# One address phase for all weights, and 256-column products in the gate and the second output half

## The chip, the core and the metric

The kernel runs on one core of a Trainium2 chip. The metric is the device time of one execution, in microseconds (us). TensorE (PE in the profile) multiplies: each product is a weight load (PEld) of a 128 x 128 block and a MATMUL that streams an operand of up to 512 columns past it into PSUM. VectorE is DVE, ScalarE is ACT, GpSimd is POOL, SyncE is SP. SBUF is the on-chip memory of 128 partitions; addresses here are bytes within a partition.

## What is computed

Two layers of an encoder on 256 positions of width 2048, in float32. Cut to what matters:

```python
for i in range(DEPTH):                       # 2
    u = _rmsnorm(h, norm_g[i]) @ w_in[i]     # 2048 -> 5632
    a_val, a_glu, a_z, q, k, v, b_z = jnp.split(u, offs, axis=-1)
    ya = _conformer_conv(a_val, a_glu, ...) * jax.nn.silu(a_z)
    yb = _window_attention(q, k, v, bias_band, sink[i]) * jax.nn.silu(b_z)
    h = h + jnp.concatenate([ya, yb], axis=-1) @ w_out[i]
    e = _rmsnorm(p[i] @ w_pe[i], pe_g[i])
    h = h + e * jax.nn.sigmoid(h @ w_pg[i])
return _rmsnorm(h, final_g)
```

## The kernel before

Activations are kept transposed: features on the partitions in 16 tiles of 128, the 256 positions along the free dimension. To keep float32 accuracy with the fast float32r products, every operand is held as two parts, `hi` (the value cast to float32r) and `lo` (what the cast left over), and a product is the sum of three: w_hi x_hi, w_hi x_lo and w_lo x_hi. The operand tiles (`hg` for the normed input, `ya` and `yb` for the two head groups, `h1` for the residual) have the shape [128, 2, 8, 256]: hi and lo, eight feature tiles, 256 positions.

The weights stream from HBM in halves of [128, 1024] float32, 156 a layer. Two halves come with one DMA (`load`, on SP). `split` (lines 163 to 172) turns one half into a `w` tile that holds hi (ACT, line 169) and then lo (DVE, line 172), up to `LS` = 4 halves ahead of their use. There are five such buffers, one for each tag `w0` to `w4`, used in turn; each is 2 x 1024 + 16 elements long, 8256 bytes, and the data begin `SHIFT[i]` elements after its start, with `SHIFT = (0, 2, 4, 8, 16)` (line 52). Half h uses the tag h modulo 5. The allocator puts the five buffers one after another, `w4` first, at a multiple of 64 bytes; the operand tiles are 16384 bytes each.

`step` (line 420) takes the next half, runs its eight slices of 128 x 128 through `mm3`, and then calls `pump`, which issues what is due of the side work: convolution taps on DVE, one stage of an attention head, and so on. Side work therefore stands between the steps on every engine, in an order that is fixed by the program for DVE, PE and ACT.

`mm3` (line 398) has two forms. With a two-dimensional output it makes three products of 256 columns (lines 405 to 407). With a three-dimensional output it makes two (lines 402 and 403): w_hi against hi and lo side by side, 512 columns into a whole PSUM bank, and w_lo against hi, 256 columns, into the bank's second half. In this wide form the two halves of the bank must be added afterwards.

A layer runs: `e` (the embedding, `w_pe`), `ag` (value and gate of the convolution), `k`, `v`, then for each pair of head tiles `zb` and `q`, with attention as side work, then `za`, the output projection and the gate. Attention's own products are the scores (line 648), the transposes (line 675) and probabilities times values (line 685). The layernorm of the convolution group adds products at lines 724, 355 and 369 while the first half of the output projection runs.

The output projection is done in two passes. The first takes the attention half of the weights (`yb`) in the narrow form, two output tiles to a bank, and adds the bank into `az` (line 772). The second takes the convolution half (`ya`) in the wide form, a bank for each output tile, with two adds each (line 784), and splits the result into `h1` (lines 785 and 786).

The gate (`w_pg`) uses the wide form through `wide` (line 445); `merge` (line 409) adds the halves of a bank, an ACT copy (line 413) and a DVE add (line 414), and `gate` (line 800) applies the sigmoid, multiplies, adds and squares. Only the last tile of the last layer was already in the narrow form. `pair` (line 438), the narrow form for two tiles in one bank, serves the input projection.

Of the kernel before, what the change touches and what calls it, by code (L numbers as in the profile page):

```python
# [10 lines left out]
F32 = mybir.dt.float32  # L11
F32R = mybir.dt.float32r
# [5 lines left out]
P = 128  # L18
D = 2048
S = 256  # L20
DEPTH = 2
KT = D // P
# [16 lines left out]
HALF = 1024  # L39
# [9 lines left out]

NB_FIRST = KT  # L50
NSPL = 5
SHIFT = (0, 2, 4, 8, 16)
MAN = 'DVE,PE,Activation'
LY = (2, 1)
ORD = 1
# [74 lines left out]
def trunk_kernel(ctx: ExitStack, tc: tile.TileContext, xT, pT, wst, par, gain, relb, sinkp, onehot, out):  # L130
    nc = tc.nc
# [2 lines left out]
        ctx.enter_context(tc.manual_schedule(engines={getattr(ET, x) for x in MAN.split(",")}))  # L134
    big = ctx.enter_context(tc.tile_pool(name="big", bufs=5))
    wraw = ctx.enter_context(tc.tile_pool(name="wraw", bufs=3))
    wspl = ctx.enter_context(tc.tile_pool(name="wspl", bufs=1))
    cst = ctx.enter_context(tc.tile_pool(name="cst", bufs=1))
    wk = ctx.enter_context(tc.tile_pool(name="wk", bufs=2))
    ps = ctx.enter_context(tc.tile_pool(name="ps", bufs=8, space=PSUM))  # L140
# [2 lines left out]
    def bigt(name, dt=F32):  # L143

        return big.tile([P, 2, 8, S], dt, tag="big", name=name)

    def halves(t):
        return [t[:, 0], t[:, 1]]

    def bank(name):  # L150
        return ps.tile([P, 2, S], F32, tag="ps", name=name)
# [10 lines left out]

    def split(h):
        raw = raws[h // 2][:, h % 2, :]
        i = h % NSPL
        w = wspl.tile([P, 2 * HALF + 16], F32R, tag=f"w{i}", name=f"w{h}")
        w = w[:, SHIFT[i]:SHIFT[i] + 2 * HALF].rearrange("p (t n) -> p t n", t=2)
        hi, lo = w[:, 0], w[:, 1]
        nc.scalar.copy(hi, raw)  # L169
        spl[h] = w  # L170
        if h not in (4, 5):
            nc.vector.tensor_sub(lo, raw, hi.bitcast(F32))  # L172
# [17 lines left out]
    def get(h):  # L190

        r = h % NHALF
        if r < 12:
            ahead(h + (r | 1) + 2 - r)
        else:
            ahead(h + LS)
        return spl.pop(h)
# [31 lines left out]
    def later(f, *args):  # L229

        def g():
            f(*args)
            return
            yield

        side.append(g())
# [43 lines left out]
    h = halves(bigt("x"))  # L280
# [104 lines left out]
    def square_acc(acc, src, first, eng=None):  # L385

        if first:
            nc.scalar.activation(acc, src, AF.Square)
            return
        sq = wk.tile([P, 2, S], F32, name="sq", tag="sq", bufs=3)  # L390
        nc.scalar.activation(sq, src, AF.Square)
        (eng or nc.gpsimd).tensor_add(acc, acc, sq)
# [5 lines left out]
    def mm3(o, w, x, start, stop):  # L398


        if len(o.shape) == 3:
            nc.tensor.matmul(o, w[:, 0], x, start=start, stop=False, skip_group_check=True)  # L402
            nc.tensor.matmul(o[:, 1], w[:, 1], x[:, 0], start=False, stop=stop, skip_group_check=True)  # L403
            return
        nc.tensor.matmul(o, w[:, 0], x[:, 0], start=start, stop=False, skip_group_check=True)  # L405
        nc.tensor.matmul(o, w[:, 0], x[:, 1], start=False, stop=False, skip_group_check=True)  # L406
        nc.tensor.matmul(o, w[:, 1], x[:, 0], start=False, stop=stop, skip_group_check=True)  # L407

    def merge(bs):

        t = wk.tile([P, 2, S], F32, name="hl", tag="ptt")[:, 0:len(bs), :]
        for x, b in enumerate(bs):
            nc.scalar.copy(t[:, x, :], b[:, 1, :])
            nc.vector.tensor_add(t[:, x, :], b[:, 0, :], t[:, x, :])
        return t

    class Cursor:
        h = 0

    def step(o, X, start, stop):  # L420

        steps([o], X, [start], stop)

    def steps(os, X, starts, stop):

        parts = []
        for _ in os:
            name, _, k0, nk = HALVES[Cursor.h % NHALF]
            parts.append(get(Cursor.h).rearrange("p t (k c) -> p t k c", k=nk))
            Cursor.h += 1  # L430
        for kk in range(nk):
            k = k0 + kk
            for o, w, start in zip(os, parts, starts):
                mm3(o, w[:, :, kk, :], X[k // 8][:, :, k % 8, :], start and kk == 0, stop and kk == nk - 1)
        for _ in os:
            pump()

    def pair(X, name):
        b = bank(name)
        for x in range(2):  # L440
            step(b[:, x, :], X, x == 0, False)
            step(b[:, x, :], X, False, True)
        return b

    def wide(X, name):

        b = bank(name)
        step(b, X, True, False)
        step(b, X, False, True)
        return b  # L450

    def hilo(hi, lo, src):
# [5 lines left out]
    for l in range(DEPTH):  # L458
# [28 lines left out]
        for q in range(4):  # L487
            n = Cursor.h
            Cursor.h += 1
            if l:  # L490
                w = get(n).rearrange("p t (j k c) -> p t j k c", j=4, k=2)
            else:
                raw = raws[n // 2][:, n % 2, :].rearrange("p (j k c) -> p j k c", j=4, k=2)
            for jj in range(0, 4, 2):
                j = 4 * q + jj
                b = bank("e")
                for x in range(2):
                    for k in range(2):
                        if l:
                            mm3(b[:, x, :], w[:, :, jj + x, k, :], pp[:, :, k, :], x == 0 and k == 0, k == 1)  # L500
                        else:
                            nc.tensor.matmul(b[:, x, :], raw[:, jj + x, k, :], pf[:, k, :], start=x == 0 and k == 0,
                                             stop=k == 1, skip_group_check=True)
# [89 lines left out]
        for ts in FIRST_TILES:  # L593
            bs = [bank(f"ag{l}_{t}") for t in ts]
# [14 lines left out]
        b = pair(hg, f"k{l}")  # L609
# [9 lines left out]
        for q in range(4):  # L619
            n = Cursor.h  # L620
            Cursor.h += 1
            w = get(n).rearrange("p t (k c) -> p t k c", k=4)
# [67 lines left out]
        for i in range(0, 8, 2):  # L690

            b = pair(hg, f"zb{l}_{i}")
            nc.scalar.activation(zb[:, i:i + 2, :], b, AF.Silu)
            b = pair(hg, f"q{l}_{i}")

            qq = wk.tile([P, 2, 2, S], F32R, name="qq", tag="qq")
            for hh in range(2):
                r, o = rows_of[hh], rows_of[1 - hh]
# [7 lines left out]
        for t in range(0, NCT, 2):  # L706
            b = pair(hg, f"za{l}_{t}")
# [55 lines left out]
        Y = [ya, yb]  # L763
        for k in (0, 4):
            nc.gpsimd.dma_start(zb[:, k:k + 4, :], hsrc[:, 8 + k:12 + k, :])
        h1 = []
        for j in range(0, KT, 2):
            b = bank(f"o{l}_{j}")
            for x in range(2):
                step(b[:, x, :], Y, x == 0, True)  # L770
            d = az[:, j // 8, j % 8:j % 8 + 2, :]
# [3 lines left out]
        for j in range(0, KT, 2):  # L775
            d = az[:, j // 8, j % 8:j % 8 + 2, :]
            if j % 8 == 0:
                h1.append(bigt(f"h1{l}_{j // 8}", F32R))
            hi, lo = (x[:, j % 8:j % 8 + 2, :] for x in halves(h1[-1]))
            for x in range(2):  # L780
                b = bank(f"o{l}_{j + x}")
                step(b, Y, True, True)
                for y in range(2):
                    nc.vector.tensor_add(d[:, x, :], b[:, y, :], d[:, x, :])
            nc.scalar.copy(hi, d)
            sub = lambda d=d, hi=hi, lo=lo: nc.vector.tensor_sub(lo, d, hi.bitcast(F32))
            if j < KT - 2:
                later(sub)
            else:
                sub()  # L790
# [3 lines left out]
        last = l == DEPTH - 1  # L794
# [5 lines left out]
        def gate(j, b):  # L800

            i, jj, n = j // 8, j % 8, b.shape[1]
            hh, hl = (x[:, jj:jj + n, :].bitcast(F32) for x in halves(h1[i]))
            hs = wk.tile([P, 2, S], F32, name="hs", tag="u", bufs=3)[:, 0:n, :]
            nc.vector.tensor_add(hs, hh, hl)
            sg = wk.tile([P, 2, S], F32, name="sg", tag="sq", bufs=3)[:, 0:n, :]
            nc.scalar.activation(sg, b, AF.Sigmoid)
            d = e[i][:, jj:jj + n, :]
            nc.vector.tensor_mul(d, d, sg)
            nc.vector.tensor_add(d, d, hs)  # L810
            if n == 2:
                square_acc(hacc, d, j == 0)
            else:
                sq = wk.tile([P, 2, S], F32, name="sq", tag="sq", bufs=3)[:, 0, :]
                nc.scalar.activation(sq, d[:, 0, :], AF.Square)
                if j == KT - 1:
                    hparts.append(sq)
                else:
                    hparts.append(fold(hacc))
                    nc.vector.tensor_add(hparts[0], hparts[0], sq)  # L820
            if last:
                for x in range(n):
                    nc.scalar.activation(og[i][:, jj + x, :], e[i][:, jj + x, :], AF.Copy,
                                         scale=gcol(DEPTH, j + x))
            elif jj + n == 8:
                nc.gpsimd.dma_start(hscr[:, 8 * i:8 * i + 8, :], e[i])
# [4 lines left out]
        hparts = []  # L831
        for j in range(0, KT - 2, 2):
            if j:
                bs = [wide(h1, f"g{l}_{j + x}") for x in range(2)]
            else:
                bs = [bank(f"g{l}_{x}") for x in range(2)]
                for n in range(2):
                    for b in bs:
                        step(b, h1, n == 0, n == 1)
            gate(j, merge(bs))  # L840
            if j == 4 and not last:
                pp = wk.tile([P, 2, 2, S], F32R, name="pp", tag="qq")
                hilo(pp[:, 0], pp[:, 1], pf)
        for j in range(KT - 2, KT):
            if last and j == KT - 1:
                b = bank(f"g{l}_{j}")[:, 0:1, :]
                step(b[:, 0, :], h1, True, False)
                step(b[:, 0, :], h1, False, True)
                gate(j, b)
            else:  # L850
                gate(j, merge([wide(h1, f"g{l}_{j}")]))
        drain()
        h = e

# [7 lines left out]
    for j in (0, 2, 12, 4, 6, 14, 8, 10):  # L862
        for x in [slice(0, 1), slice(1, 2)] if j == 0 else [slice(0, 2)]:
            d = og[j // 8][:, j % 8:j % 8 + 2, :][:, x, :]
# [82 lines left out]
```

## Time and profile before

| what | us |
|---|---|
| runs shown: lowest, median, highest | 963.55, 966.16, 966.61 |
| profiled execution, its time | 963.42 |
| its span, first to last instruction | 961.7 |
| mean granted TensorE clock | 0.997 of full speed |
| MATMULs in the span | 7216 |

The profile comes from one execution. Its page gives the busy time of each engine, the span in 40 slices, the chain of work that ended last and the costliest groups of instructions; the timeline gives the start of each instruction. MATMULs overlap: the next one starts long before the duration shown for the last one is over, so the distance between starts is what fills the span.

### The profile page before, as it was taken

The numbers are of one execution on the slowest core, as the hardware profiler recorded it, in microseconds if no ns is written. First come the engines' busy times: TensorE is split into PE (matmuls) and PEld (weight loads), VectorE is DVE, ScalarE is ACT, GpSimd is POOL, SyncE is SP. The second block draws the span as 40 slices with busy tenths as digits, with TensorE's granted clock in tenths as the row PEclk, the third lists the DMA queues.
The fourth block names the chain that finished last, engine by engine and source line by source line (L and its number), as shares of the span: only waits on it lengthen the run. The fifth ranks groups of instructions, "written<-read, shape, count | busy, mean of one in ns | idle before, by whom it ended". The sixth has DMA issues, their size and how long they took to land.

```text
span 961.7 us, 17740 instructions
## 1 busy us (share of the span) xinstructions
PE 948.5 (99%) x7216; PEld 897.8 (93%) x7216; DVE 792.2 (82%) x1369; ACT 558.6 (58%) x861; POOL 83.6 (9%) x79
## 2 busy tenths in 40 slices
PE   8999999999999999999999999999999999999996
PEld 7999999999999998888899999999999999888885
DVE  3899989998787687887789998998887878677763
ACT  4655455777875553555566444568778545446552
POOL 0022101010000000011103200000100000000111
PEclk9999999999999999999999999999999999999998
DMA  7674546555446464546546455466454555545532
GB/s 292 224 247 175 188 164 238 197 184 188 164 160 242 153 217 165 210 175 230 204 180 220 172 198 201 176 213 206 151 172 169 190 190 193 194 168 183 178 129 88
DMA packets 29005, 182.45 MB, mean 190 GB/s; under 512 B 3595, under 2 KB 4156, under 8 KB 9084
## 3 DMA queue, kind: packets, MB, share of 16 engines
q1 hardware_dynamic: 24284, 165.70, 49.1%
q0 software_dynamic: 3344, 12.88, 4.2%
q10 hardware_dynamic: 1296, 2.75, 0.8%
q8 instruction: 56, 0.92, 0.4%
q14 instruction: 25, 0.20, 0.1%
HBM read 177.09 MB, written 4.23 MB: 189 GB/s over the span
## 4 chain that ended last, share of the span: by engine, by line
PE 94%; DVE 3%; ACT 1%; DMA 1%; issue 0%; POOL 0%; ACTq 0%; DVEq 0%
PE g L402 12%; PE o L402 6%; PE g L403 6%; PE ag L405 6%; PE ag L407 6%; PE ag L406 6%; PE za L405 3%; PE zb L405 3%; PE q L405 3%; PE o L403 3%; PE za L407 3%; PE za L406 3%; PE zb L406 3%; PE q L407 3%; PE zb L407 3%; PE q L406 3%
## 5 line engine op out<-in xcount | busy, mean ns | idle before, releaser
L172 DVE TENSOR_TENSOR w<-raw,w 128x1024 fp32r<-128x1024 f32 x306 | 373.7, 1231 | 96.0 <-ACT w L169 93.4
L169 ACT CAST w<-raw 128x1024 fp32r<-128x1024 f32 x308 | 314.1, 1048 | 142.2 <-PE ag L407 43.0
L580 DVE SCALAR_TENSOR_TENSOR cz<-az,pars,cz 128x241 f32<-128x241 f32 (+11 forms) x480 | 216.8, 501 | 1.0
L402 PE MATMUL g<-h,w 128*128 128x512 f32 x496 | 174.4, 396 | 0.0
L407 PE MATMUL ag<-hg,w 128*128 128x256 f32 x512 | 142.9, 279 | 0.5 <-DVE w L172 0.5
L405 PE MATMUL ag<-hg,w 128*128 128x256 f32 x512 | 143.3, 280 | 0.0
L406 PE MATMUL ag<-hg,w 128*128 128x256 f32 x512 | 142.7, 279 | 0.0
L403 PE MATMUL g<-h,w 128*128 128x256 f32 x496 | 139.0, 280 | 0.0
L402 PEld LDWEIGHTS g<-h,w 128*128 128x128 f32 x496 | 93.1, 188 | 22.6
L407 PEld LDWEIGHTS ag<-hg,w 128*128 128x128 f32 x512 | 96.2, 188 | 0.9 <-DVE w L172 0.9
L405 PEld LDWEIGHTS ag<-hg,w 128*128 128x128 f32 x512 | 96.2, 188 | 0.9 <-ACT w L169 0.8
L406 PEld LDWEIGHTS ag<-hg,w 128*128 128x128 f32 x512 | 96.3, 188 | 0.1
L403 PEld LDWEIGHTS g<-h,w 128*128 128x128 f32 x496 | 93.3, 188 | 0.0
L402 PE MATMUL o<-ya,w 128*128 128x512 f32 x256 | 90.1, 396 | 0.0
L405 PE MATMUL za<-hg,w 128*128 128x256 f32 x256 | 72.9, 285 | 0.0
L405 PE MATMUL q<-hg,w 128*128 128x256 f32 x256 | 72.4, 283 | 0.0
L405 PE MATMUL zb<-hg,w 128*128 128x256 f32 x256 | 72.2, 282 | 0.0
L405 PE MATMUL o<-yb,w 128*128 128x256 f32 x256 | 72.1, 282 | 0.0
L403 PE MATMUL o<-ya,w 128*128 128x256 f32 x256 | 71.7, 280 | 0.0
L407 PE MATMUL za<-hg,w 128*128 128x256 f32 x256 | 71.5, 279 | 0.0
L406 PE MATMUL za<-hg,w 128*128 128x256 f32 x256 | 71.5, 279 | 0.0
L406 PE MATMUL o<-yb,w 128*128 128x256 f32 x256 | 71.5, 279 | 0.0
(224 smaller groups left out, 2076.4 us busy)
## 6 DMA issues: line engine op xcount, KB each, us to landing
raw<-in_wst SPq DMA_DIRECT2D x153, 1024.0 KB, 4.9
bias<-fscr POOLq DMA_DIRECT2D x16, 384.0 KB, 3.8
raw<-in_wst SPq DMA_DIRECT2D x4, 512.0 KB, 8.0
az<-in_xT POOLq DMA_DIRECT2D x4, 512.0 KB, 6.1
hscr<-e POOLq DMA_DIRECT2D x2, 1024.0 KB, 5.1
az<-hscr POOLq DMA_DIRECT2D x4, 512.0 KB, 6.1
x<-in_xT SPq DMA_DIRECT2D x3, 512.0 KB, 8.3
out_t<-og ACTq DMA_DIRECT2D x4, 256.0 KB, 3.2
```

What stands on the lines that cost most here:

```text
L169: nc.scalar.copy(hi, raw)
L172: nc.vector.tensor_sub(lo, raw, hi.bitcast(F32))
L402: nc.tensor.matmul(o, w[:, 0], x, start=start, stop=False, skip_group_check=True)
L403: nc.tensor.matmul(o[:, 1], w[:, 1], x[:, 0], start=False, stop=stop, skip_group_check=True)
L405: nc.tensor.matmul(o, w[:, 0], x[:, 0], start=start, stop=False, skip_group_check=True)
L406: nc.tensor.matmul(o, w[:, 0], x[:, 1], start=False, stop=False, skip_group_check=True)
L407: nc.tensor.matmul(o, w[:, 1], x[:, 0], start=False, stop=stop, skip_group_check=True)
L580: nc.vector.scalar_tensor_tensor(acc[:, t, lo_:hi_], a[:, t, lo_ + s:hi_ + s], w(k), acc[:, t, lo_:hi_], ALU.mult, ALU.add)
```

## The change

All five weight buffers get one tag with five rotating buffers, each 2 x 1024 + 64 elements long (8448 bytes, a multiple of 128), and the data begin 16 elements (64 bytes) after the buffer's start. The wide form of `mm3`, `wide` and `merge` are gone. The second pass of the output projection puts two tiles into one bank in the narrow form and adds the bank at once. The gate uses `pair`, and `gate` reads the bank itself.

```diff
-SHIFT = (0, 2, 4, 8, 16)
+SHIFT = 16
...
-    wspl = ctx.enter_context(tc.tile_pool(name="wspl", bufs=1))
+    wspl = ctx.enter_context(tc.tile_pool(name="wspl", bufs=NSPL))
...
-        i = h % NSPL
-        w = wspl.tile([P, 2 * HALF + 16], F32R, tag=f"w{i}", name=f"w{h}")
-        w = w[:, SHIFT[i]:SHIFT[i] + 2 * HALF].rearrange("p (t n) -> p t n", t=2)
+        w = wspl.tile([P, 2 * HALF + 64], F32R, tag="w", name=f"w{h}")
+        w = w[:, SHIFT:SHIFT + 2 * HALF].rearrange("p (t n) -> p t n", t=2)
...
-        if len(o.shape) == 3:
-            nc.tensor.matmul(o, w[:, 0], x, start=start, stop=False, skip_group_check=True)
-            nc.tensor.matmul(o[:, 1], w[:, 1], x[:, 0], start=False, stop=stop, skip_group_check=True)
-            return
...
+            b = bank(f"o{l}_{j}")
             for x in range(2):
-                b = bank(f"o{l}_{j + x}")
-                step(b, Y, True, True)
-                for y in range(2):
-                    nc.vector.tensor_add(d[:, x, :], b[:, y, :], d[:, x, :])
+                step(b[:, x, :], Y, x == 0, True)
+            nc.vector.tensor_add(d, b, d)
...
             if j:
-                bs = [wide(h1, f"g{l}_{j + x}") for x in range(2)]
+                b = pair(h1, f"g{l}_{j}")
             else:
-                bs = [bank(f"g{l}_{x}") for x in range(2)]
+                b = bank(f"g{l}_{j}")
                 for n in range(2):
-                    for b in bs:
-                        step(b, h1, n == 0, n == 1)
-            gate(j, merge(bs))
+                    for x in range(2):
+                        step(b[:, x, :], h1, n == 0 and x == 0, n == 1)
+            gate(j, b)
...
         for j in range(KT - 2, KT):
-            if last and j == KT - 1:
-                b = bank(f"g{l}_{j}")[:, 0:1, :]
-                step(b[:, 0, :], h1, True, False)
-                step(b[:, 0, :], h1, False, True)
-                gate(j, b)
-            else:
-                gate(j, merge([wide(h1, f"g{l}_{j}")]))
+            b = bank(f"g{l}_{j}")[:, 0:1, :]
+            for n in range(2):
+                step(b[:, 0, :], h1, n == 0, n == 1)
+            gate(j, b)
```

More of the change, by code (lines that the diff above doesn't have):

```diff
@@ L407, in mm3 @@
         nc.tensor.matmul(o, w[:, 1], x[:, 0], start=False, stop=stop, skip_group_check=True)
[L409 to L415, printed above, removed]
     class Cursor:
@@ L442, in pair @@
             step(b[:, x, :], X, False, True)
[L443 to L449, printed above, removed]
         return b
```

## The prediction, made before the result was known

> **What bounds the kernel now.** I read the page first (busy shares, slices, chain), then the waits of PE.
>
> ```profile
> span 961.7 us, 17740 instructions
> PE 948.5 (99%) x7216; PEld 897.8 (93%) x7216; DVE 792.2 (82%) x1369; ACT 558.6 (58%) x861; POOL 83.6 (9%) x79
> PE   8999999999999999999999999999999999999996
> PEclk9999999999999999999999999999999999999998
> PE 94%; DVE 3%; ACT 1%; DMA 1%; issue 0%; POOL 0%; ACTq 0%; DVEq 0%
> ```
>
> ```profile
> PE rh0c L355 <- DVE fold L379: 1.7, 1, 1.7
> PE ag L407 <- DVE w L172: 0.5, 1, 0.5
> ```
>
> PE is the bound in every slice, at full granted clock, and its listed waits are a few us at most. So the time is the number of products times the distance from one product's start to the next; the durations listed (279 ns for a 256-column product) overlap and say nothing of that distance. I take distances from the timeline. A **step** is one weight half: 8 slices, 24 products of 256 columns (or 8 pairs of 512 and 256). Five steps in a row of the first layer begin at these rows, 24 products between each row and the next:
>
> ```profile
> 71.50 0.28 PE L405 MATMUL ag<-hg,w 128*128 128x256 f32 x1
> 74.22 0.28 PE L405 MATMUL ag<-hg,w 128*128 128x256 f32 x1
> 77.06 0.28 PE L405 MATMUL ag<-hg,w 128*128 128x256 f32 x1
> 79.86 0.28 PE L405 MATMUL ag<-hg,w 128*128 128x256 f32 x1
> 82.70 0.28 PE L405 MATMUL ag<-hg,w 128*128 128x256 f32 x1
> 85.43 0.28 PE L405 MATMUL ag<-hg,w 128*128 128x256 f32 x1
> ```
>
> These are the steps of buffers w0, w1, w2, w3, w4: 2.72, 2.84, 2.80, 2.84, 2.73 us. The pattern repeats with period five wherever nothing interrupts. From the layout of the pools (buffers 8256 bytes apart, w4 first, plus SHIFT times 4), the weights lie modulo 64 bytes at 0, 8, 16, 32, 0 from the operand tiles for w0 to w4, and modulo 128 w0 and w4 lie at 64. So the two buffers that already have the new phase keep the shorter distance, 113.3 ns a product, against 118.3, 116.6 and 118.3.
>
> But the same phase also runs slowly. Two further steps, w4 then w0, 48 products between these rows:
>
> ```profile
> 617.19 0.28 PE L405 MATMUL q<-hg,w 128*128 128x256 f32 x1
> 622.84 0.28 PE L405 MATMUL q<-hg,w 128*128 128x256 f32 x1
> ```
>
> 5.65 us / 48 = 117.8 ns, or 2.827 us a step. Counting all 85 steps of w0 and w4 through the timeline by their last twelve products, 60 run at 113.3 ns and 24 at 117.8 (one between). There are **two paces**, and wherever a w0 step follows a w4 step without a break it inherits its pace, slow or fast, save in the first layer's first steps and once after v. The off-phase buffers now break every run after two steps. After the change nothing does, save PE work of another kind between steps.
>
> **The change, part by part.** *1. Wide products go.* The second output half and the gate run as pairs:
>
> ```profile
> L402 PE MATMUL g<-h,w 128*128 128x512 f32 x496 | 174.4, 396 | 0.0
> L403 PE MATMUL g<-h,w 128*128 128x256 f32 x496 | 139.0, 280 | 0.0
> L402 PE MATMUL o<-ya,w 128*128 128x512 f32 x256 | 90.1, 396 | 0.0
> L403 PE MATMUL o<-ya,w 128*128 128x256 f32 x256 | 71.7, 280 | 0.0
> ```
>
> ```profile
> 390.74 0.40 PE L402 MATMUL g<-h,w 128*128 128x512 f32 x1
> 404.80 0.40 PE L402 MATMUL g<-h,w 128*128 128x512 f32 x1
> ```
>
> 752 pairs / 8 = 94 steps. Five of them take 14.06 us between the two rows, 2.812 each. As 24 narrow products a step takes 2.720 at the fast pace, 2.827 at the slow one: 94 x 0.092 = 8.6 us won, or 94 x 0.015 = 1.4 us lost. The 752 added products and weight loads are in these step times.
>
> The Trainium skill ("TensorE: Matmul & The Clock Gate", Back-to-back issue gap) gives an isolated gap of N/2.4 + 2.5 ns, by which I estimate 325 ns for a pair and 327.5 for the triple: the split would cost 1.9 us. The rows do not go by it: the pair takes 2.812 / 8 = 351 ns, the fast triple 340.
>
> *2. All weights at one phase.* 129 narrow steps use w1, w2, w3, mean 2.827 us: at the fast pace they win 129 x 0.107 = 13.8, at the slow one nothing. Of the w0 and w4 steps, the 24 at 117.8 ns can win 2.6, the 60 at 113.3 ns can lose 6.4. So **everything fast is 8.6 + 13.8 + 2.6 = 25.0 us less, everything slow 6.4 + 1.4 = 7.8 us more**. What I must choose is which pace each stretch takes.
>
> *3. What sets the pace.* These pairs of rows are the 12th and the 24th product of three steps at the new phase that follow attention's own products:
>
> ```profile
> 242.19 0.28 PE L407 MATMUL q<-hg,w 128*128 128x256 f32 x1
> 243.55 0.28 PE L407 MATMUL q<-hg,w 128*128 128x256 f32 x1
> ...
> 275.16 1.08 PE L685 MATMUL av<-ptt,v 128*64 128x256 f32 x8
> 277.57 0.28 PE L407 MATMUL za<-hg,w 128*128 128x256 f32 x1
> 278.99 0.28 PE L407 MATMUL za<-hg,w 128*128 128x256 f32 x1
> ...
> 636.35 0.28 PE L407 MATMUL zb<-hg,w 128*128 128x256 f32 x1
> 637.71 0.28 PE L407 MATMUL zb<-hg,w 128*128 128x256 f32 x1
> ```
>
> The first follows the transposes (L675) and runs 1.36 / 12 = 113 ns; the second follows the probability products (L685), 1.42 / 12 = 118; the third follows the scores (L648), 113. Where the step before the break also had the new phase, this repeats: fast to slow after L685 in four of four, fast after L675 in three of three, fast after L648 in two of two, from either pace. In attention's rhythm of four steps (after L685, after L648, after L675, no break) one step in four is then slow: 88 steps / 4 x 0.107 = 2.4 us given back of the 25.0.
>
> The other stretches are long and have one entry each. The last 10 steps of the first output half, the second half and the gate make 58 steps a layer, entered after the broadcasts of L369. The one entry there at the new phase goes fast, but it comes from another phase. I take them as fast; each costs 58 x 0.107 = 6.2 us if not. The 104 steps of the layers' starts, ag, k, v and the first heads have entries of unlike kinds: I take half of them slow, 5.6 us. Sum: -25.0 + 2.4 + 5.6 = **-17.0**.
>
> *4. Merges and adds.* Off PE these go, or change:
>
> ```profile
> L413 ACT COPY hl<-g 128x256 f32<-128x256 f32 x31 | 11.5, 370 | 19.1 <-PE g L403 19.1
> L414 DVE TENSOR_TENSOR hl<-g,hl 128x256 f32<-128x256 f32 x31 | 12.2, 418 | 5.6 <-ACT hl L413 5.6
> L784 DVE TENSOR_TENSOR az<-o,az 128x256 f32<-128x256 f32 x64 | 27.0, 422 | 2.0 <-PE o L403 0.9
> L772 DVE TENSOR_TENSOR az<-o,az 128x512 f32<-128x512 f32 x16 | 11.0, 686 | 1.1 <-PE o L407 1.1
> ```
>
> The 64 adds become 16 of the last row's kind: DVE is freed of 12.2 + 27.0 - 11.0 = 28.2 us, ACT of 11.5. I cost both at nothing, because PE never paused there:
>
> ```profile
> 60.30:113.28 52.98, 52.98 (x458) 52.98 (x457) 52.91 (x83) 26.11 (x33) 14.51 (x8) 1.00 0.56 194
> 345.75:480.74 134.99, 134.99 (x771) 117.50 (x770) 104.08 (x148) 67.62 (x89) 8.39 (x7) 1.00 0.57 202
> ```
>
> (Window, its length, busy PE, PEld, DVE, ACT, POOL, clock, DMA.) In the second window, output and gate, DVE has 31 us to spare already. At a layer's end the gate is 0.37 + 0.42 = 0.8 us earlier; other products cover that in the first layer, and the very last tile was never merged. At most 1.6 us, taken as 0. No wait is added, no DMA or queue is moved, and buffers are still recycled five steps later.
>
> *5. Does DVE keep up?* The first window, ag, has DVE busy 52.91 of 52.98 us, so a faster PE eats the lead of the low halves (L172). The narrowest places:
>
> ```profile
> 542.28 1.21 DVE L172 TENSOR_TENSOR w<-raw,w 128x1024 fp32r<-128x1024 f32 x1
> 546.74 0.28 PE L407 MATMUL ag<-hg,w 128*128 128x256 f32 x1
> ...
> 807.43 1.23 DVE L172 TENSOR_TENSOR w<-raw,w 128x1024 fp32r<-128x1024 f32 x1 [0.25 <-ACT w L169]
> 810.13 0.28 PE L407 MATMUL o<-yb,w 128*128 128x256 f32 x1
> ```
>
> Leads of 546.74 - 543.49 = 3.25 us and 810.13 - 808.66 = 1.47 us. In ag at most 27 steps of 0.07 us on average, 1.9 us, are won before DVE next idles: covered. The layernorm place loses some 0.4: covered, barely. At the start PE already waits for DVE (the 0.5 us above): I drop 0.3 us there. If the cover fails, up to 2 us a layer are lost.
>
> The profiled execution took 963.42 us (span 961.7 and 1.7 around it); the runs shown are 963.55, 966.16 and 966.61, so it lies at their lower end. 963.4 - 17.0 + 0.3 = 946.7; half of the 2.7 us to the median added, **948**.
>
> **Rivals.** *A. Long stretches lock slow.* One of the two 58-step stretches slow: 948 + 6 = 954; both: 960. For it: L685 leaves slow, and the layernorm's mean (L724) comes just before these stretches. Against it: the one entry seen after L369.
>
> *B. Slow everywhere, slower than before.* If the slow pace is what an unbroken run at this phase falls into, w1 to w3 win nothing, w0 and w4 lose theirs: 963.4 + 7.8 = 971, 974 against the median. It decides if more than three quarters (25.0 of 32.8) of all steps run slow. For it: the first steps and 622 us are slow with no off-phase buffer between. Against it: two of attention's three breaks lead to fast.
>
> *C. The phase is not the cause.* Then narrow steps keep their mean pace of (2.72 + 2.84 + 2.80 + 2.84 + 2.73) / 5 = 2.786, the 94 wide steps win 0.026 each: -2.4, 961 (964 against the median). Against it: the rows by buffer, whose order repeats exactly. The Trainium skill ("SBUF — State Buffer", Who interferes with whom) gives PE two independent read ports and names only the pair shared by DVE and GpSimd as contended; by that rule the shift would do nothing. The 0.12 us between w0's and w1's steps speak against it.
>
> *D. Fast everywhere.* 963.4 - 25.0 = 938, if the phase makes every entry fast.
>
> **How the numbers follow.** Both long stretches fast 0.47 (942 to 952, by how the 104 steps fall); A with one slow 0.20, both 0.13; D 0.07; B 0.07; C 0.06. The range runs from 940, short of D, to 962, past A and C. A measurement here tells about 0.3% (2.9 us). Faster: the first, A and D, with part of C, 0.86; within 0.3%: the rest of C and the upper end of A, 0.08; slower: B and what else I miss, 0.06.
>
> **What would show it.** Lines 402, 403, 413 and 414 gone, 7968 products, step starts 2.72 us apart through the gate. Slow stretches 2.827 apart with no break inside would be A or B. Steps still alternating by buffer would be C. Wrong altogether if PE waits for L172 in ag, or if a pace changes within a run without a break.

## The result, and the profile after

The changed kernel took 954.82 us in the median of 8 runs (945.92 to 959.84), the kernel before 964.50 in 8 (963.55 to 966.61); the ratio is 0.9895 with a 95% interval of 0.9859 to 0.9932. It is faster by 1%, and its runs spread over 14 us where those of before spread over 3. The profiled execution is the longest of the eight, 959.84 us with a span of 958.1.

From the page of the changed kernel: span, busy time, PE and its clock in the 40 slices, the chain, and the gate's products; the last row is from PE's waits.

```profile
span 958.1 us, 19136 instructions
PE 944.6 (99%) x7968; PEld 927.4 (97%) x7968; DVE 769.2 (80%) x1290; ACT 549.9 (57%) x830; POOL 80.9 (8%) x79
PE   8999999999999999999999999999999999999996
PEclk9999999999999999999999999999999999999998
PE 95%; DVE 3%; DMA 1%; issue 0%; ACT 0%; POOL 0%; ACTq 0%; DVEq 0%
L400 PE MATMUL g<-h,w 128*128 128x256 f32 x512 | 143.9, 281 | 0.0
L402 PE MATMUL ag<-hg,w 128*128 128x256 f32 x512 | 142.2, 278 | 0.6 <-DVE w L171 0.5
```

```profile
PE ag L402 <- DVE w L171: 0.5, 1, 0.5
```

The wide products and the merges are gone, there are 7968 products, PE is still busy in every slice at the full clock, and it waits no more for DVE than before. What fills the span is again the distance between starts. The windows view shows it in two stretches of the first layer: 20 steps of ag, and the 58 steps from the layernorm's broadcasts to the end of the gate (window, length, busy PE, PEld, DVE, ACT, POOL, clock, DMA):

```profile
61.37:115.77 54.40, 54.40 (x483) 54.40 (x482) 54.33 (x86) 27.11 (x34) 12.82 (x8) 1.00 0.55 192
315.99:480.02 164.03, 164.03 (x1395) 164.03 (x1394) 114.59 (x135) 80.53 (x97) 8.40 (x7) 1.00 0.55 193
```

54.40 / 20 = 2.720 us a step: every buffer now has the short pace of 113.3 ns there, although DVE is busy all the time. 164.03 / 58 = 2.828: the output and the gate run at the long pace of 117.8 ns from end to end, and the same 164.03 us come back in the second layer. These 58 steps took 162.9 us before. So in this execution the stretches that should have given most gave 1.1 us a layer away; ag and k (from the tenth step on) won 1.8 and 0.7, attention 1.5 and 1.8, and the remaining stretches 1.1 together. The start of the first ag step, 25.30 us against 24.08, costs 1.2. This is not the change's doing: in this execution the granted clock is halved for 3.4 us before that step (0.50, third number from the end), and `e9_fill`, which keeps the whole change, starts at 23.8 without such a stretch.

```profile
18.00:21.40 3.40, 3.40 (x11) 2.77 (x11) 1.39 (x2) 2.40 (x4) 0.71 (x1) 0.50 0.71 279
```

Over the 14 profiles the first ag step starts between 23.8 and 24.3 us where no such stretch is, between 25.3 and 25.8 where it lasts 3.4 us, and between 27.2 and 27.5 where it lasts 6.8. Up to 3.7 us of the difference between two executions can come from there. Counted through the timeline, 124 of 308 steps end at the short pace, 179 at the long one.

### The profile page after: what moved, and what is told of

The parts are those of the page before. It is cut to its first block, busy times and chain, and to the rows that moved or that the text cites. A ratio compares the mean times of both kernels' runs of the same rounds, so it can differ in the third digit from the quotient of the medians.

```text
span 958.1 us, 19136 instructions
## 1 busy us (share of the span) xinstructions
PE 944.6 (99%) x7968; PEld 927.4 (97%) x7968; DVE 769.2 (80%) x1290; ACT 549.9 (57%) x830; POOL 80.9 (8%) x79
## 4 chain that ended last, share of the span: by engine, by line
PE 95%; DVE 3%; DMA 1%; issue 0%; ACT 0%; POOL 0%; ACTq 0%; DVEq 0%
PE g L401 6%; PE g L400 6%; PE g L402 6%; PE ag L402 6%; PE o L401 6%; PE ag L400 6%; PE o L400 6%; PE o L402 6%; PE ag L401 6%; PE za L400 3%; PE zb L400 3%; PE q L400 3%; PE za L401 3%; PE za L402 3%; PE zb L401 3%; PE q L401 3%
## 5 line engine op out<-in xcount | busy, mean ns | idle before, releaser
L400 PE MATMUL g<-h,w 128*128 128x256 f32 x512 | 143.9, 281 | 0.0
L401 PE MATMUL g<-h,w 128*128 128x256 f32 x512 | 143.9, 281 | 0.0
L402 PE MATMUL g<-h,w 128*128 128x256 f32 x512 | 143.9, 281 | 0.0
L402 PEld LDWEIGHTS g<-h,w 128*128 128x128 f32 x512 | 97.2, 190 | 0.0
L400 PEld LDWEIGHTS g<-h,w 128*128 128x128 f32 x512 | 97.2, 190 | 0.0
L401 PEld LDWEIGHTS g<-h,w 128*128 128x128 f32 x512 | 96.1, 188 | 0.0
L400 PE MATMUL za<-hg,w 128*128 128x256 f32 x256 | 72.6, 284 | 0.0
L400 PE MATMUL o<-ya,w 128*128 128x256 f32 x256 | 71.9, 281 | 0.0
L401 PE MATMUL o<-ya,w 128*128 128x256 f32 x256 | 71.9, 281 | 0.0
L402 PE MATMUL o<-ya,w 128*128 128x256 f32 x256 | 71.9, 281 | 0.0
```

## The experiments

Every kernel was compared with runs of the kernel before on the same chip. "Short" and "long" are the paces of 113.3 and 117.8 ns a product.

**One half of the change at a time.** `e1_phase_only` keeps the wide form and has only the new buffers (`SHIFT = 16`, one tag). `e2_narrow_only` has the narrow gate and output with the five old phases.

> The phase change alone; gate and second output half stay wide. Theory (a run at one phase keeps the pace it was entered with, 113.3 or 117.8 ns a product): ag steps 2.72 us for all buffers, wide steps near 2.82 as before, so only what the other stretches won in the profile of the changed kernel, about 5 us: 958 to 961. If the phase is not the cause: narrow steps still alternate by buffer, 964.

> Narrow gate and second output half alone, weight buffers at the five old phases. Theory: each buffer keeps its own distance there too, 2.72, 2.84, 2.80, 2.84, 2.72 us a step, 94 x 0.026 = 2.4 us less: 962. If the output and gate stretch is slow for a reason of its own (its operand tiles, its traffic): every step there about 2.83, w0 and w4 too, 966.

Measured: 958.23 us (ratio 0.9943, 0.9925 to 0.9960) and 962.22 (0.9982, 0.9973 to 0.9991), both as the theory had them. Step starts in the gate, first `e1_phase_only`, then `e2_narrow_only`, five steps between each two rows:

```profile
389.60 0.40 PE L401 MATMUL g<-h,w 128*128 128x512 f32 x1
403.73 0.40 PE L401 MATMUL g<-h,w 128*128 128x512 f32 x1
```

```profile
391.83 0.28 PE L401 MATMUL g<-h,w 128*128 128x256 f32 x1
405.75 0.28 PE L401 MATMUL g<-h,w 128*128 128x256 f32 x1
```

14.13 / 5 = 2.826 us for a wide step at the new phase, no better than at the old ones, and 13.92 / 5 = 2.784 for narrow steps at the five old phases. Narrow products alone win 2.3 us, and the new phase alone wins nothing in the gate. So the 58 x 0.107 = 6.2 us between a long and a short stretch can only be had from both together.

**Which phase.** `e8_phase_32` and `e11_phase_0` move all five buffers:

```diff
-SHIFT = 16
+SHIFT = 8       # e8_phase_32; 0 in e11_phase_0
```

> The changed kernel with the data 32 bytes, not 64, behind the buffer's start, so all weights off the 64-byte boundary as w3 was. If the distance modulo 64 sets the pace: every narrow step 2.84 us, none at 2.72, no jumps between two paces, 970 to 973 with a spread below 4 us. If the phase is not the cause: as the changed kernel, 946 to 960.

> The changed kernel with the data at the buffer's start, so weights at the operands' own phase modulo 256 bytes, still on a 64-byte boundary. If only the distance modulo 64 bytes matters: the same two paces, 113.3 and 117.8 ns, and times as the changed kernel, 946 to 960. If the 64 bytes past the operands are what gives the short pace: no step at 2.72, 966 or more.

Measured: 974.56 us (1.0114, 1.0100 to 1.0128) and 986.03 (1.0229, 1.0215 to 1.0243). First five gate steps of `e8_phase_32`, then 11 ag steps of `e11_phase_0`:

```profile
396.16 0.28 PE L400 MATMUL g<-h,w 128*128 128x256 f32 x1
410.36 0.28 PE L400 MATMUL g<-h,w 128*128 128x256 f32 x1
```

```profile
55.00 0.28 PE L400 MATMUL ag<-hg,w 128*128 128x256 f32 x1
86.68 0.28 PE L400 MATMUL ag<-hg,w 128*128 128x256 f32 x1
```

2.840 us a step and 31.68 / 11 = 2.880, that is 118.3 and 120.0 ns. No step of either runs at 113.3 ns: counted through the timelines, the steps of `e8_phase_32` lie between 118.0 and 118.8 (116.7 at v, where weights and operand change places), those of `e11_phase_0` between 119.3 and 120.0, the very first step and the embedding's steps of the second layer aside. The runs spread over 2 to 3 us. The first came out 1.6 us above the expected range. The second refutes my reduction modulo 64 bytes: at distance 0 a product costs 6.7 ns more than the short pace at 64. What counted in w0 and w4 was then their 64 bytes modulo 128.

These runs move the weights alone, so they could as well show the weights' own address. One place of the changed kernel speaks for the distance: the embedding's steps of the second layer stream another operand, `pp`, past the same five buffers, and the first of them, 24 products, takes 2.88 us, 120.0 ns a product, between these rows.

```profile
480.02 0.28 PE L400 MATMUL e<-pp,w 128*128 128x256 f32 x1
482.90 0.28 PE L400 MATMUL e<-pp,w 128*128 128x256 f32 x1
```

In `e11_phase_0` the same steps run at 117 ns, where nearly all others run at 120.0. No run moved an operand tile on purpose.

**What decides between the two paces.** I counted, in four profiled executions at the new phase (the changed kernel, e1, e3, e4), which pace follows which break, from the step before:

| products between two steps | from short | from long |
|---|---|---|
| none | short 358 | long 451, short 4 (v to zb) |
| scores | short 12 | short 52 |
| transposes | short 56 | short 8 |
| probabilities times values | long 64 | not seen |
| one-column sums (rv, re) | short 8 | short 8 |
| broadcasts, embedding (re) | long 8 | not seen |
| broadcasts, layernorm (rv) | long 2, short 2 | not seen |
| layernorm's mean | not seen | long 7, short 1 |

(The row rv leaves out e3 and e4, which add products there. Left out too are the embedding's own steps, the one break by the attention bias's product, and the first nine steps of each layer: there gaps of 0.22 to 0.80 us stand inside steps, and five times the pace behind such a gap is another, seven times it is the same.) All but the layernorm's rows and the step from v to zb look lawful. Five kernels put something behind those broadcasts to force the short pace on the 58 steps:

```diff
             rb = rstd_row(dg, f"rv{l}")
+            kick(yb)      # kick() in e5 and e6
```

`kick` (its body is cut here) makes n products into a scrap bank:

- e3: 4 of float32r, 256 columns of `yb`, both operands 32 bytes off the boundary
- e4: 4 of the same, on the boundary
- e5: 8 of float32, one column
- e6: 8 float32 transposes of 128 columns
- e7: 4 of float32, 256 columns

> The changed kernel plus four 256-column products into a scrap bank right behind the layernorm's broadcasts, with both operands starting 32 bytes off a 64-byte boundary. Theory (the entry decides, and products off the phase leave quick, as the scores do): both 58-step stretches at 2.72 us a step in every execution, 945 to 950, and a spread below 6 us. If the stretch itself is slow: no change, about 955 with the same spread of 14 us.

> The same four products with both operands on the 64-byte boundary. Theory: they only prolong the run and leave the pace to chance: about 955, spread like that of the changed kernel. If any products without a wait behind the broadcasts set the pace: like the off-phase ones, 945 to 950.

> The changed kernel plus eight one-column float32 products into a scrap bank behind the layernorm's broadcasts. New theory (the kind of product that ended last before a run sets its pace: one-column products, scores and transposes leave it quick, broadcasts leave it mostly slow): both 58-step stretches at 2.72 us a step in every execution, 944 to 949, spread below 6 us, eight products cost under 1 us a layer. If chance at any break sets it: about 955, spread 14 us.

> Eight float32 transposes of 128 columns at the same place in their stead. New theory: as with the columns, 944 to 949. If only one-column products do it, or chance: about 955 with a wide spread.

> Four float32 products of 256 columns at the same place, the kind that attention's probability products are. New theory: both stretches slow, 2.827 us a step, in every execution, 958 to 962, spread below 6 us. If any extra product between the broadcasts and the run makes it quick: 944 to 949; if chance: about 955.

Measured: 956.14 us (950.78 to 962.90), 954.69 (953.04 to 956.66), 957.66 (950.96 to 964.70), 958.38 (953.93 to 963.96) and 958.09 (950.85 to 963.70). None had one time; four spread over 10 to 14 us. In the profiles e3 has both stretches long, e4, e6 and e7 one long and one short, e5 both short. So neither the first theory (off-phase products reset the pace) nor the second (the last kind of product sets it) holds at this place; e4 came out where the first had it, but a median of 955 is also what chance gives, and its spread of 3.6 us in four runs shows that four runs alone tell little of the spread. e5 besides lost time of its own, told at the end.

What sets the layernorm's broadcasts apart from the embedding's is in the timeline of the changed kernel: first the embedding's (line 368, `re0b`), then the layernorm's (`rv0b`), with the products around them.

```profile
127.00 0.28 PE L402 MATMUL k<-hg,w 128*128 128x256 f32 x1
127.11 0.60 PE L368 MATMUL re0b<-ident,re0col 128*128 128x128 f32 x4
127.47 0.36 PE L400 MATMUL v<-w,hg 128*128 128x256 f32 x1
```

```profile
314.93 0.28 PE L400 MATMUL o<-yb,w 128*128 128x256 f32 x1
315.52 0.71 PE L368 MATMUL rv0b<-ident,rv0col 128*128 128x128 f32 x4
315.99 0.36 PE L400 MATMUL o<-yb,w 128*128 128x256 f32 x1
```

The embedding's follow 0.11 us after a product; from the last product before to the first behind they take 475 or 476 ns in every profile at the new phase. The layernorm's start 0.36 us after the last product of the step (315.16), because PE stands until POOL has the column (the profile lists a wait of 0.3 us of the weight load of `rv0b` for `rv0col`); the gap from product to product is 830 and 835 ns here, 828 and 834 in e1. After that wait the pace differed. The third theory: a real wait of PE sets its phase anew, and with it the pace, and everything that follows without a wait only carries that chance on. To test it the wait has to go, by work and not by removing it: ten products on `yb`, which is ready, before the broadcasts (`e9_fill`), and in `e10_fill_transposes` four transposes behind them too.

```diff
+    def fill(y, n=10):
+        kb = bank("fill")
+        for _ in range(n):
+            nc.tensor.matmul(kb[:, 0, :], y[:, 0, 0, 0:P], y[:, 0, 0, :], start=True, stop=True)
...
+            fill(yb)
             rb = rstd_row(dg, f"rv{l}")
+            turn()      # e10 alone: 4 x nc.tensor.transpose(kb[:, 0, 0:P], ones, ident)
```

> The changed kernel plus ten in-phase 256-column products before the layernorm's broadcasts, so that PE does not stand waiting for their column; nothing behind them. Theory now (a real wait of PE sets the fine phase anew, and so the pace by chance; without a wait each kind of break leads always to the same pace): the gap at the broadcasts no longer varies, and both 58-step stretches take the same pace in every execution, slow as after the embedding's broadcasts, which never wait: 958 to 962, spread below 6 us. If chance at any break: 946 to 962 with a spread of about 14 us.

> The same ten products before the broadcasts and four transposes behind them. Theory now: no wait, and transposes that follow no wait have always left the run quick, so both stretches at 2.72 us a step in every execution, 946 to 950, spread below 6 us. If chance at any break: 947 to 963 with a wide spread, like the transposes alone (954 to 964).

Measured: **960.81 us** (959.20 to 961.91, five runs) and **949.64** (948.64 to 951.08, four runs), ratios 0.9962 (0.9950 to 0.9975) and 0.9852 (0.9837 to 0.9868). The windows of the 58 steps in both layers, first `e9_fill`, then `e10_fill_transposes`, and the place itself in the latter's timeline:

```profile
314.98:479.01 164.03, 164.03 (x1395) 164.03 (x1394) 114.36 (x134) 80.54 (x97) 8.38 (x7) 1.00 0.53 192
779.50:943.52 164.02, 164.02 (x1395) 164.02 (x1394) 107.12 (x130) 82.25 (x107) 7.75 (x6) 1.00 0.45 161
```

```profile
317.01:474.87 157.86, 157.86 (x1396) 157.86 (x1395) 113.95 (x134) 80.38 (x97) 8.38 (x7) 1.00 0.55 198
775.80:933.66 157.86, 157.86 (x1395) 157.86 (x1394) 107.08 (x130) 81.97 (x107) 7.75 (x6) 1.00 0.46 166
```

```profile
315.01 1.36 PE L380 MATMUL fill<-yb 128*128 128x256 f32 x10
316.21 0.60 PE L368 MATMUL rv0b<-ident,rv0col 128*128 128x128 f32 x4
316.65 0.60 PE L386 MATMUL turn<-ident,ones 128*128 128x128 f32 x4
317.01 0.37 PE L412 MATMUL o<-yb,w 128*128 128x256 f32 x1
```

With the wait filled, the spread of the runs shrinks to 2.7 and 2.4 us, all five times of `e9_fill` lie where two long stretches put them and all four of `e10_fill_transposes` where two short ones do, and in both profiles the pace follows the table: long behind the broadcasts, short behind transposes. The ten products lengthen the gap by 0.84 us (832 to 1672 ns). The transposes cost another 0.44 (to 2108 ns) and win 164.03 - 157.86 = 6.17 us a layer; 2 x (6.17 - 0.44) = 11.5 us, and the medians differ by 11.2. e10 beats both kernels: 949.64 against 954.82 and 964.60.

Could the ten products themselves, and not the missing wait, have fixed the pace? e9 alone does not exclude it. For the wait speak the embedding's broadcasts, which have neither a wait nor added products before them: in the nine profiles at 64 bytes (the changed kernel, e1, e3 to e7, e9, e10) all 18 of them, entered from a short step, leave the pace long. The ten products give one more figure on the phase: both their operands start at the same address, and they lie 120 ns apart (1.20 us from 315.01 to 316.21), as the steps of `e11_phase_0` do at distance 0.

The other half of the theory, that a break without a wait always leads to the same pace, fails at the layernorm's mean (line 704 of the changed kernel). These rows are from the first and the second layer of `e9_fill`: the last product before the mean, the first two of its six products, the first product behind them, and the starts of the second and the fifth step.

```profile
294.18 0.28 PE L414 MATMUL za<-hg,w 128*128 128x256 f32 x1
294.30 0.59 PE L716 MATMUL mean<-ysum,ones 128*128 128x256 f32 x2
295.41 0.47 PE L412 MATMUL o<-yb,w 128*128 128x256 f32 x1
298.49 0.28 PE L412 MATMUL o<-yb,w 128*128 128x256 f32 x1
306.97 0.28 PE L412 MATMUL o<-yb,w 128*128 128x256 f32 x1
...
759.17 0.28 PE L414 MATMUL za<-hg,w 128*128 128x256 f32 x1
759.29 0.59 PE L716 MATMUL mean<-ysum,ones 128*128 128x256 f32 x2
760.40 0.47 PE L412 MATMUL o<-yb,w 128*128 128x256 f32 x1
763.43 0.28 PE L412 MATMUL o<-yb,w 128*128 128x256 f32 x1
771.59 0.28 PE L412 MATMUL o<-yb,w 128*128 128x256 f32 x1
```

The mean begins 0.12 us after a product, and no wait of PE is in it: from the last product before to the first behind it takes 1228 or 1229 ns in all 18 passages of the nine profiles, always from a long step. Yet the three steps between the last two rows take 8.48 us (2.827 each, long) in the first layer and 8.16 (2.720, short) in the second. Of the 18 passages 12 come out long and 6 short. Five steps a layer, 0.5 us, hang on it. So a wait is one way by which the pace comes to differ between executions, and not the only one.

**Further bits of the address.** `e12_phase_192` is e10 with `SHIFT = 48`.

> The kernel with ten products before and four transposes behind the broadcasts, but the data 192 bytes behind the buffer's start instead of 64. If the pattern repeats every 128 bytes: the same paces, 948 to 951. If it repeats only every 256 bytes or later: another distance than 113.3 and 117.8 ns in the ag steps, and a time outside that range.

Measured: 968.73 us (1.0045, 1.0029 to 1.0061). Neither branch was right as a whole: the paces are those of the first, the time lies where the second had it. The steps have the same two paces, but other breaks lead to them. Ten steps of ag in the second layer take 2.720 us each, and the 58 steps behind the transposes are long:

```profile
530.59:557.79 27.20, 27.20 (x242) 27.20 (x241) 27.20 (x44) 13.04 (x16) 4.27 (x3) 1.00 0.54 192
320.99:485.02 164.03, 164.03 (x1395) 164.03 (x1394) 114.45 (x134) 80.42 (x97) 8.41 (x7) 1.00 0.54 191
```

Attention's transposes, which left the run short in all 64 cases of the table at 64 bytes, leave it long in all 16 here. So at both distances that are 64 modulo 128 there is this pair of paces, and which of them a break chooses differs between 64 and 192 bytes.

## Why the prediction was right, and where it was off

*The bound and the terms.* Right: PE's distances between starts carry the time, and there are two paces at the new phase. The prices of a step, 2.720 and 2.827 us, came back within 0.001 in windows of 20 and 58 steps. The start of a w0 or w4 step that follows the scores was seen short three times in the profile of before, not two; that changes nothing. By the isolated gap of N/2.4 + 2.5 ns in the Trainium skill ("TensorE: Matmul & The Clock Gate", Back-to-back issue gap) the split was estimated to cost 1.9 us; the runs do not agree, `e2_narrow_only` wins 2.3.

*The phase (rival C).* Excluded by e8 and e11, where a constant alone takes the ag steps to 2.83 to 2.85 and to 2.88 us, and none runs at 2.72. By the Trainium skill's rule ("SBUF — State Buffer", Who interferes with whom), that only the port pair shared by DVE and GpSimd is contended, the shift would do nothing; the runs do not agree, 974.56 and 986.03 us.

*Attention.* Right in kind: in every cycle of four steps one is long, the one after the probability products. But 32 of the 88 steps are long, not 22, about 1 us more: in each layer eight follow the probability products, three more follow these without a break, at the last heads, where no scores come between, and five stand behind the layernorm's mean, which the prediction gave no price.

*The 104 other steps.* Half long was assumed, 52; 31 are in the profiled execution, 2.2 us better. That is luck: no row of the prediction fixed this term.

*The long stretches.* This is the step that was mis-sized: "I take them as fast; each costs 58 x 0.107 = 6.2 us if not." The price was right (164.03 - 157.86 = 6.17), the choice was not. The one entry seen in the profile of before followed the layernorm's broadcasts, where PE waits, and one such entry is no rule. In the profiled execution both stretches are long, 959.84 us, as rival A had it with both. From there one long stretch would give 953.7 and none 947.5, and the runs cover all three, with what the start of an execution adds or takes. The case that was held likeliest, both short at 942 to 952, holds two of the eight times (951.88 and 945.92). The median of 954.82 stands where rival A with one long stretch had it, 954: the range held because it reached past A, and that the median lies inside it is in part the luck of eight executions. How many stretches are long in the seven unprofiled ones is inferred from their times alone.

*Merges, DVE.* Right: the merges and adds that went (28 us of DVE and 11 of ACT by their rows; the page's busy sums fell by 23.0 and 8.7) show nowhere in the time; ag runs at 2.720 a step with DVE busy all the time.

*B and D* did not come. But something like B exists: at 192 bytes 250 of 308 steps are long, and 968.73 us are more than before, though about 2.6 of them (2 x (0.84 + 0.44)) are the products that e10 adds.

*The sign of a pace that changes within a run without a break* did come, once in every profile at 64 bytes: from v to zb in the second layer the pace goes from long to short with no product between. The prediction had seen a change after v once in the profile of before; that a run keeps its pace needs this exception. At v the weights are the streamed operand and `hg` is the loaded one.

## What to carry to other kernels

When PE is busy all the time, measure the distance between starts, by buffer: the phase of the weights against the streamed operand was worth 0.16 us of a 2.88 us step here, and no busy share shows it. When two paces exist, ask what sets the pace at the head of each long run, and look whether PE waits there: a break that always led to one pace can be built for, while behind the wait here either pace came. A spread of runs that grows with a change is such a sign. Filling the wait alone made the spread small and the kernel slower (960.81 us against 954.82); filling it and putting behind it the kind of product that leads to the short pace won another 5 us, half of what the change had won.

## What was not expected of the hardware

Four distances for one product, 256 columns with a 128-column weight load, by the weights' distance from the operands: 113.3 or 117.8 ns at 64 bytes modulo 128, 118.0 to 118.8 at 32, 120.0 at 0. Why the two paces exist, how a wait chooses, and what differs between two passages of the layernorm's mean, no run here shows.

In `e5_kick_columns`, eight one-column products, two passes each, stand where the granted clock fell, in both layers. The windows of that kernel around the first of the two places (clock is the third number from the end):

```profile
311.00:317.70 6.70, 6.13 (x52) 5.93 (x51) 4.66 (x7) 1.32 (x2) 1.63 (x1) 0.96 0.85 313
317.70:320.80 3.10, 3.10 (x17) 3.10 (x17) 0.26 (x1) 1.09 (x2) 0.00 (x0) 0.53 0.00 0
```

The clock is 0.53 for 3.1 us, in which 17 products start where the long pace has 26. From the last full product before to the first behind, 3.10 us pass here (3.09 in the second layer), in which PE waits 0.57 us, makes the four broadcasts and then the sixteen passes of one column. In `e7_kick_wide_float32`, with eight passes of 256 columns at the same place, the same stretch takes 2.45 and 2.92 us, and the clock stays at full. So products of one column did not keep the clock up here, though the engine counts as busy; what part the wait before them has, no run separates.
